# Expert stage of a hybrid backbone: TensorE in written order, gather and combination inside gate and up, and two adjacent weight rows of each 256 on a partition

## The chip, the cores and the metric

The kernel runs on one core of a Trainium2 chip. The metric is the device time of one execution in microseconds (us). A core has five engines, each with an instruction queue of its own that is worked off in order: TensorE (PE, matrix products; its weight loads are listed as PEld), VectorE (DVE), ScalarE (ACT), GpSimd (POOL) and SyncE (SP), which here mainly issues DMAs. Sixteen DMA engines move data between the memory outside (DRAM) and the core's own (SBUF). Matrix products land in PSUM.

## The reference

One layer of a backbone with a token-mixing half and an expert half, on 512 tokens of width 2048. Only the expert half concerns the change. Every token chooses one of four expert groups and two of the eight experts in it; an expert is a gated MLP of width 512:

```python
def _hier_moe(h, w_rg, b_rg, w_re, b_re, w_gate, w_up, w_down):
    # top-1 group, top-2 experts in it, weights wts; slots sorted by expert
    ...
    def expert_block(args):
        idx, e = args
        xb = h_pad[idx]
        return (jax.nn.silu(xb @ w_gate[e]) * (xb @ w_up[e])) @ w_down[e]
    ys = lax.map(expert_block, (buf_tok.reshape(n_blocks, MOE_BLOCK), blk_e))
    ys = ys.reshape(cap, d) * buf_w[:, None].astype(h.dtype)
    return jax.ops.segment_sum(ys, buf_tok, num_segments=t + 1)[:t]
```

Here `h` is the modulated, normalised stream (512 x 2048). The result is scaled by a row of modulation (`gt2`), added to the stream, and the stream is normalised once more for the output. All 32 experts' weights (32 x 3 matrices of 2048 x 512 in f32, 403 MB) are read in every run.

## The kernel before

The first two thirds of the kernel (modulation, input projection, three recurrent mixers, output projection) stay as they are. `out_more` loads two rows of the modulation, spread over all partitions, into `as2`; `route_tile` and `route_h2` multiply and add them to make `h2` (128 partitions x 4 token tiles x 2048). `route_slots` chooses the experts. Then comes `phase_moe`, the expert stage.

An expert's tokens are gathered into 64 slots. The work of the stage:

- `gather(q)` serves four experts at once ("quad" below). It makes a one-hot matrix `G` (tokens x 4 x 64 slots) on VectorE and multiplies `h2` by it on TensorE, in 16 chunks of 128 features. Each chunk is split into a rounded part `hh` (cast by ScalarE) and a rest `hl` (subtracted by VectorE, for odd chunks by GpSimd), each with two buffers; a chunk is 8 matmuls of 256 columns (L1685), and after two chunks VectorE copies the PSUM tile (`pc_`, three buffers) to `xg` (L1686). `xg` is one tile with one buffer.
- `gate_up(e)` multiplies the 64 slots by gate and up together: 16 features-chunks x 2 column halves = 32 matmuls into `pgu` (L1716). The halves `c` go to different 64-column parts of TensorE. ScalarE applies silu, VectorE multiplies (`sil_`).
- `turn(e)` transposes the activation (L1728) to `hT`.
- `down(pr, cols)` multiplies a pair of experts by w_down, 8 matmuls for each of four column blocks of 512 (L1740, `py`); VectorE scales (`yt`), ScalarE rounds (`yeh`), VectorE takes the rest (`yel`).
- `slots(pr)` makes the pair's one-hot matrix, its transpose `GT` (L1698, L1699) and the slots' weights (L1702).
- `combine()` adds a column block to the stream `x1`: for four token tiles two matmuls with `GT` into `pc_` (L1763) and an addition on VectorE (L1764).

A f32 matmul of `pgu` or `py` leaves two records in the trace, so one expert's gate/up has 64, and the profile's "x8" is four matmuls.

The weights go through a ring of ten slots of 1 MB (`slot`, `load`): each gate/up slot holds two feature rows of gate and of up on each partition, each down slot two row blocks. `load()` is called when a slot has been read; SyncE issues the DMA when the slot's last reader is done. SyncE's queue is in order.

What sets the order: the instructions of an engine are put in order by a list scheduler at build time, which takes ready work by priority, so the order in the program is not that of the source. In the stage before, a quad's gather runs while its first expert's gate/up runs, chunk by chunk ahead of it.

## Time and profile before

| | |
|---|---|
| median of 3 runs | 3124.62 us (3121.7 to 3134.05) |
| profiled execution | 3124.07 us; span from first to last instruction 3122.3 us |
| PE busy | 2810.3 us (90%) |
| DVE, ACT, POOL busy | 1633.1, 859.9, 812.2 us |
| DMA | 730.79 MB, mean 234 GB/s |
| one quad in the stage, 2261.60 to 2397.60 | PE busy 130.34 of 136.00 us, DMA 370 GB/s |
| gate/up matmuls (L1716) | 2048 records, 487.1 us busy |
| down matmuls (L1740) | 1024 records, 257.0 us busy |

Times of single instructions are counted from the span's start. "Busy" of TensorE includes the modelled ends of matmuls, so a stretch can be busy and still not dense. Rows of a wait name who waited and, behind the arrow, what came last. The expert stage begins at about 2010 us and lasts to the end.

### The profile page before, as it was taken

The numbers are of one execution on the slowest core, as the hardware profiler recorded it, in microseconds if no ns is written. First come the engines' busy times: TensorE is split into PE (matmuls) and PEld (weight loads), VectorE is DVE, ScalarE is ACT, GpSimd is POOL, SyncE is SP. The second block draws the span as 40 slices with busy tenths as digits, with TensorE's granted clock in tenths as the row PEclk, the third lists the DMA queues.
The fourth block names the chain that finished last, engine by engine and source line by source line (L and its number), as shares of the span: only waits on it lengthen the run. The fifth ranks groups of instructions, "written<-read, shape, count | busy, mean of one in ns | idle before, by whom it ended". The sixth has DMA issues, their size and how long they took to land. (4 is left out here: it accounts for less than half of the span.)

```text
span 3122.3 us, 50607 instructions
## 1 busy us (share of the span) xinstructions
PE 2810.3 (90%) x19241; PEld 1825.2 (58%) x19241; DVE 1633.1 (52%) x3215; ACT 859.9 (28%) x1570; POOL 812.2 (26%) x765
## 2 busy tenths in 40 slices
PE   5989998988989989889789888799999999999997
PEld 3478777777677766667556666644344343434432
DVE  4275657685675554455375656624343342434335
ACT  4142332346432233222132332412122120212202
POOL 2232222221433432433343443411011010101101
PEclk9999999989999999999989899899999999999999
DMA  8767878887543443443383323499999999999996
GB/s 305 272 191 217 248 221 265 246 258 210 136 110 97 104 108 98 105 107 82 103 266 98 116 70 100 154 365 369 409 342 385 362 343 410 342 409 342 382 369 247
DMA packets 526878, 730.79 MB, mean 234 GB/s; under 512 B 121042, under 2 KB 343808, under 8 KB 525220
## 3 DMA queue, kind: packets, MB, share of 16 engines
q1 hardware_dynamic: 362832, 640.77, 57.9%
q10 hardware_dynamic: 161927, 81.17, 10.2%
q0 software_dynamic: 1872, 5.57, 0.6%
q8 instruction: 154, 2.52, 0.3%
q14 instruction: 93, 0.75, 0.1%
HBM read 672.50 MB, written 54.93 MB: 233 GB/s over the span
## 5 line engine op out<-in xcount | busy, mean ns | idle before, releaser
L1716 PE MATMUL pgu<-ring,xg 128*64 128x512 f32 x2048 | 487.1, 599 | 0.0
L307 POOL TENSOR_TENSOR wl<-wr,wh 128x512 fp32r<-128x512 f32 x191 | 263.8, 1382 | 666.9 <-ACT wh L306 606.9
L329 PE MATMUL pl<-hil,wh 128*128 128x512 f32 x928 | 404.2, 436 | 4.6 <-ACT hil L241 3.7
L329 PE MATMUL pl<-lol,wh 128*128 128x512 f32 x928 | 375.9, 405 | 0.2
L329 PE MATMUL pl<-hil,wl 128*128 128x512 f32 x928 | 371.5, 400 | 1.1 <-POOL wl L307 1.1
L306 ACT CAST wh<-wr 128x512 fp32r<-128x512 f32 x292 | 179.6, 619 | 532.2 <-PE pl L329 290.6
L1682 POOL TENSOR_TENSOR hl<-h,hh 128x512 fp32r<-128x512 f32 x64 | 99.4, 1554 | 861.7 <-ACT hh L1681 861.7
L1716 PEld LDWEIGHTS pgu<-ring,xg 128*64 128x64 f32 x2048 | 137.3, 136 | 254.1 <-issue 236.0
L1740 PE MATMUL py<-ring,hT 128*64 128x512 f32 x1024 | 257.0, 598 | 0.0
L259 DVE SCALAR_TENSOR_TENSOR acc<-w,sil,acc 128x512 f32<-128x512 f32 x240 | 201.4, 868 | 55.6 <-DMA w<-in_w_ada_dram 54.0
L329 PEld LDWEIGHTS pl<-hil,wh 128*128 128x128 f32 x928 | 178.9, 193 | 60.5 <-issue 15.1
L329 PEld LDWEIGHTS pl<-hil,wl 128*128 128x128 f32 x928 | 178.7, 193 | 42.2 <-POOL wl L307 1.8
L329 PEld LDWEIGHTS pl<-lol,wh 128*128 128x128 f32 x928 | 179.7, 194 | 38.1 <-issue 6.4
L1681 ACT CAST hh<-h 128x512 fp32r<-128x512 f32 x128 | 134.4, 1092 | 120.1 <-PE pc__20645 L1685 2.7
L1740 PEld LDWEIGHTS py<-ring,hT 128*64 128x64 f32 x1024 | 85.8, 136 | 129.7 <-issue 125.1
L329 PE MATMUL pc<-hic,wl 128*128 128x256 f32 x496 | 146.0, 295 | 12.9 <-DVE wl L307 8.7
L329 PE MATMUL pc<-hic,wh 128*128 128x256 f32 x496 | 145.8, 295 | 5.9 <-ACT hic L241 3.2
L329 PE MATMUL pc<-loc,wh 128*128 128x256 f32 x496 | 144.9, 293 | 1.2 <-DVE loc L242 1.2
L1748 DVE SCALAR_TENSOR_TENSOR yt<-py,Wsl,g 128x512 f32<-128x512 f32 x64 | 48.1, 751 | 161.1 <-PE py L1740 158.4
L1749 ACT CAST yeh<-yt 128x512 fp32r<-128x512 f32 x64 | 39.6, 619 | 290.0 <-DVE yt L1748 290.0
L1410 POOL TENSOR_TENSOR wol<-wo,woh 128x512 fp32r<-128x512 f32 x56 | 76.0, 1361 | 160.3 <-PE acc L1413 100.6
L776 DVE TENSOR_TENSOR ptm<-Tm,Lay 64x1 f32<-64x1 f32 (+2 forms) x270 | 106.9, 396 | 16.9 <-DMA Lay<-s_ad 10.2
(2216 smaller groups left out, 5074.9 us busy)
## 6 DMA issues: line engine op xcount, KB each, us to landing
ring<-in_moe_w_gate_dram SPq DMA_DIRECT2D x256, 512.0 KB
ring<-in_moe_w_up_dram SPq DMA_DIRECT2D x256, 512.0 KB
ring<-in_moe_w_down_dram SPq DMA_DIRECT2D x128, 1024.0 KB
wr<-in_w_in_dram ACTq DMA_DIRECT2D x288, 256.0 KB
w<-in_w_ada_dram SPq DMA_DIRECT2D x256, 256.0 KB
w<-in_w_ada_dram SPq DMA_DIRECT2D x64, 512.0 KB
wo<-in_w_out_dram SPq DMA_DIRECT2D x56, 256.0 KB
rv_xk<-d_xk SPq DMA_DIRECT2D x36, 256.0 KB
```

The costliest lines, as they stand in the source:

```text
L259: nc.vector.scalar_tensor_tensor(acc, w, self.sil[:, k, 0:1], acc, op0=OP.mult, op1=OP.add)
L306: nc.scalar.copy(wh[:, :, :n], wr[:, :, :n])
L307: (nc.vector if q in self.wdve else nc.gpsimd).tensor_tensor(wl[:, :, :n], wr[:, :, :n], wh[:, :, :n].bitcast(F32), op=OP.subtract)
L329: nc.tensor.matmul(o[:n], a[:, k, :n], r, start=(q == k == i == 0), stop=(q == k == 3 and i == 2))
L776: nc.vector.tensor_tensor(pt_[:, :t, :t], Tm[:, :t, :t], Lay[:, :t, t].rearrange("q (o s) -> q o s", o=1).to_broadcast([64, t, t]), op=OP. ...
L1410: nc.gpsimd.tensor_tensor(wl, w, wh.bitcast(F32), op=OP.subtract)
L1681: nc.scalar.copy(hh, h)
L1682: (nc.gpsimd if k else nc.vector).tensor_tensor(hl, h, hh.bitcast(F32), op=OP.subtract)
L1716: nc.tensor.matmul(p[64 * c:64 * c + 64], x[:, k, 64 * (e % 4):64 * (e % 4) + 64], g[:, :, k % 2, 256 * c:256 * c + 256], start=(k == 0), ...
L1740: nc.tensor.matmul(py[64 * c:64 * c + 64], ht[2 * pr + c][:, f % 2, 64 * (f // 2):64 * (f // 2) + 64], wgt[2 * pr + c, (col[0] // 1024, f ...
L1748: nc.vector.scalar_tensor_tensor(yt, py, W, self.g2[:, col[0]:sum(col)], op0=OP.mult, op1=OP.mult)
L1749: nc.scalar.copy(yh, yt)
```

## The change

It does five things.

1. Every matmul and transpose of the stage is kept in the order in which the code writes it (`pin`, by the helpers `mm` and `tr`; in the profile all their instructions then have the helper's line). The other engines are still ordered by the scheduler.
2. The code is written in the wanted order: `gate_up(e, *work)` takes a list of (j, call) and makes the call behind feature pair j. The calls are steps of the gather (always two at once: 32 matmuls), the transpose of the expert before, the two parts of `slots`, and two combinations. The gather of the next four experts now begins inside the last gate/up of the quad (two pairs of steps) and ends inside the next one's (two more). For the first quad three steps stand before the first gate/up.
3. `xg` becomes eight tiles of two chunks, `xg0` to `xg7`, so that each can be written again as soon as its own readers are done. `as2`, which shares their memory, is cut into eight tiles, loaded by eight DMAs in place of two.
4. A gate/up slot now holds 256 consecutive rows of the matrix, rows 2p and 2p+1 of them on partition p, in place of rows 16p+2c and 16p+2c+1. Each DMA still moves 4 KB to a partition, now from 512 KB that lie together. The gather takes the matching features: every second column of a block of 256 (step 2) in place of every 16th.
5. `combine` takes the oldest column block and not the newest.

```diff
     def out_more(self):
-        self.as2 = self.xgp.tile([P, 2, D], F32, name="as2", tag="xg")
-        self.row_bc(self.as2[:, 0], 2)
-        self.row_bc(self.as2[:, 1], 1)
+        self.as2 = [[self.xgp.tile([P, 512], F32, name=f"as2_{j}{q}", tag=f"xg{4 * j + q}") for q in range(4)] for j in range(2)]
+        for j, ts in enumerate(self.as2):
+            for q, t in enumerate(ts):
+                self.nc.sync.dma_start(t, self.d_ada[1, 2 - j:3 - j, 512 * q:512 * q + 512].to_broadcast([P, 512]))
...
-                nc.sync.dma_start(w[:, j], I[nm][0, e].rearrange("(p k) c -> p k c", p=P)[:, 2 * c:2 * c + 2])
+                nc.sync.dma_start(w[:, j], I[nm][0, e, 2 * c * P:(2 * c + 2) * P].rearrange("(p k) c -> p k c", k=2))
...
+            pin = tc.keep_in_program_order
+            def mm(*a, **k):
+                pin(nc.tensor.matmul(*a, **k))
...
             def gather(q):
-                x = xg[q] = self.xgp.tile([P, KT, 256], F32, name="xg")
+                xg[q] = []
                 yield
                 for k0 in range(0, KT, 2):
+                    x = self.xgp.tile([P, 2, 256], F32, name=f"xg{k0 // 2}")
+                    xg[q].append(x)
                     p = ps.tile([P, 2, 256], F32, name="pc_", bufs=3)
                     for k in range(2):
-                        h = self.h2[:, :, k0 + k::KT]
+                        h = self.h2[:, :, k0 * P + k:(k0 + 2) * P:2]
...
-            def gate_up(e, gat=iter(())):
+            def gate_up(e, *work):
...
+                    load()
+                    for at, call in work:
+                        if at == j:
+                            call()
...
-                pr, col, yh, yl = ys.pop()
+                pr, col, yh, yl = ys.pop(0)
...
             for pr in range(NE // 2):
                 a = 2 * pr
-                gate_up(a, gather(pr // 2) if pr % 2 == 0 else iter(()))
-                if pr:
-                    down(pr - 1, COLS[:2])
-                else:
-                    slots(0)
-                turn(a)
-                gate_up(a + 1)
-                if pr:
-                    down(pr - 1, COLS[2:])
-                    slots(pr)
-                turn(a + 1)
-            down(pr, COLS)
-            combine()
+                sl = slots(pr)
+                if pr == 0:
+                    gat = gather(0)
+                    for _ in range(4):
+                        next(gat)
+                    gate_up(a, *((j, partial(next, gat, None)) for j in range(5)))
+                else:
+                    two = () if pr % 2 else ((0, partial(next, gat)),) * 2 + ((4, partial(next, gat)),) * 2
+                    gate_up(a, *two, (1, partial(turn, a - 1)), (2, combine), (5, combine))
+                    for col in COLS[:2]:
+                        down(pr - 1, col)
+                two = ()
+                if pr % 2 and a + 2 < NE:
+                    gat = gather(pr // 2 + 1)
+                    next(gat)
+                    two = ((3, partial(next, gat)),) * 2 + ((6, partial(next, gat)),) * 2
+                next(sl)
+                gate_up(a + 1, (0, partial(turn, a)), (1, combine), (2, partial(next, sl)), *two, (4, partial(next, sl)), (5, combine))
+                if pr:
+                    for col in COLS[2:]:
+                        down(pr - 1, col)
+            turn(a + 1)
+            combine()
+            combine()
+            for i, col in enumerate(COLS):
+                down(pr, col)
+                if i:
+                    combine()
+            combine()
```

How instructions move, at three places. First TensorE around the combination behind a pair's first two down blocks (`pc_<-yeh,GT` and `pc_<-yel,GT` are the combination's two matmuls, `pgu` gate/up, `ts<-ident,sil` the activation's transpose). Before:

```order
L1763 MATMUL pc__21745<-yel,GT 128x512
L1716 MATMUL pgu<-ring_21640,xg 64x512
L1763 MATMUL pc__21749<-yeh,GT 128x512
L1763 MATMUL pc__21749<-yel,GT 128x512
L1716 MATMUL pgu<-ring_21640,xg 64x512 x3
L1763 MATMUL pc__21851<-yeh,GT 128x512
L1763 MATMUL pc__21851<-yel,GT 128x512
L1716 MATMUL pgu<-ring_21647,xg 64x512 x4
```

One gate/up matmul stands alone between two parts of a combination, and three follow. At the same kind of place now:

```order
L1672 MATMUL pgu<-ring_21462,xg_21184 64x512 x4
L1675 MATMUL ts<-ident,sil__21586 128x128 x2
L1672 MATMUL pgu<-ring_21485,xg_21211 64x512 x4
L1672 MATMUL pc__21654<-yeh,GT 128x512
L1672 MATMUL pc__21654<-yel,GT 128x512
L1672 MATMUL pc__21658<-yeh,GT 128x512
L1672 MATMUL pc__21658<-yel,GT 128x512
...
L1672 MATMUL pgu<-ring_21492,xg_21282 64x512 x4
```

The combination's eight matmuls now stand together, and gate/up comes by four.

Second TensorE at a quad's gather (`pc_<-G,hh` and `pc_<-G,hl`, four matmuls for each part of a chunk). Before, inside the first gate/up of the quad:

```order
L1685 MATMUL pc__22172<-G,hh 128x256 x4
L1685 MATMUL pc__22172<-G,hl 128x256 x4
L1716 MATMUL pgu<-ring_21944,xg 64x512 x4
L1685 MATMUL pc__22172<-G,hh 128x256 x4
L1685 MATMUL pc__22172<-G,hl 128x256 x4
L1685 MATMUL pc__22205<-G,hh 128x256 x4
L1685 MATMUL pc__22205<-G,hl 128x256 x4
L1716 MATMUL pgu<-ring_21951,xg 64x512 x4
```

Now, the second block of four chunks in the same gate/up:

```order
L1672 MATMUL pgu<-ring_21279,xg_21393 64x512 x4
L1672 MATMUL pc__21496<-G,hh 128x256 x4
L1672 MATMUL pc__21496<-G,hl 128x256 x4
L1672 MATMUL pc__21496<-G,hh 128x256 x4
L1672 MATMUL pc__21496<-G,hl 128x256 x4
L1672 MATMUL pc__21523<-G,hh 128x256 x4
L1672 MATMUL pc__21523<-G,hl 128x256 x4
L1672 MATMUL pc__21523<-G,hh 128x256 x4
L1672 MATMUL pc__21523<-G,hl 128x256 x4
L1672 MATMUL pgu<-ring_21340,xg_21420 64x512 x4
```

Two chunks between gate/up groups have become four, in four blocks a quad in place of eight.

Third ScalarE from the last expert of a quad to the first of the next (`hh` the gather's casts, `sil` the activation, `yeh` the down's rounding, `hT` the transposed activation). Before:

```order
L1749 CAST yeh<-yt 128x512
L1681 CAST hh<-h_19608 128x512 x16
L1721 ACTIVATE sil__22337<-pgu 128x256
L1749 CAST yeh<-yt 128x512 x2
L1730 COPY hT_22415<-ts 128x256
```

Now:

```order
L1692 CAST hh<-h_19621 128x512 x8
L1736 ACTIVATE sil__22144<-pgu 128x256
L1764 CAST yeh<-yt 128x512 x2
L1692 CAST hh<-h_19621 128x512 x4
L1745 COPY hT_22257<-ts 128x256
L1692 CAST hh<-h_19621 128x512 x4
```

The sixteen casts of a gather stood in one run and now stand in three, around the activation and the rounding; both kernels' first run of casts in the stage is 18 long.

More of the change, by code (lines that the diff above doesn't have):

```diff
@@ L1684, in gather @@
                             for t in range(4):
-                                nc.tensor.matmul(p[:, k], hx[:, t], G[:, t].rearrange("p e s -> p (e s)"), start=(i == t == 0), stop=(i == 1 and t == 3))
-                    nc.vector.tensor_copy(x[:, k0:k0 + 2], p)
+                                mm(p[:, k], hx[:, t], G[:, t].rearrange("p e s -> p (e s)"), start=(i == t == 0), stop=(i == 1 and t == 3))
+                    nc.vector.tensor_copy(x, p)
                     yield
@@ L1705, in slots @@
                 gts[pr] = (GT, W)
-            def gate_up(e, gat=iter(())):
-                next(gat, None)
+                yield
+            def gate_up(e, *work):
                 x = xg[e // 4]
                 p = ps.tile([P, 2, 256], F32, name="pgu", bufs=2)
-                for k in range(KT):
-                    if k % 2 == 0:
-                        next(gat, None)
-                    g = wgt[e, k // 2]
-                    for c in range(2):
-                        nc.tensor.matmul(p[64 * c:64 * c + 64], x[:, k, 64 * (e % 4):64 * (e % 4) + 64], g[:, :, k % 2, 256 * c:256 * c + 256],
-                                         start=(k == 0), stop=(k == KT - 1), tile_position=(0, 64 * c))
-                    if k % 2:
-                        load()
+                for j in range(KT // 2):
+                    g = wgt[e, j]
+                    for k in range(2):
+                        for c in range(2):
+                            mm(p[64 * c:64 * c + 64], x[j][:, k, 64 * (e % 4):64 * (e % 4) + 64], g[:, :, k, 256 * c:256 * c + 256],
+                               start=(j == k == 0), stop=(j == 7 and k == 1), tile_position=(0, 64 * c))
+                    load()
+                    for at, call in work:
+                        if at == j:
+                            call()
                 s_ = mo.tile([P, 256], F32, name="sil_", bufs=2)
@@ L1727, in turn @@
                 for j in range(2):
[L1728 removed]
+                    tr(pt[:, j], hm[e][:, j * P:(j + 1) * P], self.ident)
                 ht[e] = mo.tile([P, 2, P], F32, name=f"hT{e % 2}", bufs=2 - e % 2)
@@ L1731, in turn, with down @@
                 del hm[e]
-            def down(pr, cols):
+            def down(pr, col):
                 W = gts[pr][1]
-                for col in cols:
-                    n = col[1]
-                    py = ps.tile([P, n], F32, name="py", bufs=2)
-                    for f in range(4):
-                        for c in range(2):
-                            nc.tensor.matmul(py[64 * c:64 * c + 64], ht[2 * pr + c][:, f % 2, 64 * (f // 2):64 * (f // 2) + 64], wgt[2 * pr + c, (col[0] // 1024, f // 2)][:, f % 2, col[0] % 1024:col[0] % 1024 + n],
-                                             start=(f == 0), stop=(f == 3), tile_position=(0, 64 * c))
-                    if col[0] % 1024:
-                        for _ in range(4):
-                            load()
-                    yt = mo.tile([P, n], F32, name="yt", bufs=1)
-                    yh = mo.tile([P, n], F32R, name="yeh", bufs=2)
-                    yl = mo.tile([P, n], F32R, name="yel", bufs=2)
-                    nc.vector.scalar_tensor_tensor(yt, py, W, self.g2[:, col[0]:sum(col)], op0=OP.mult, op1=OP.mult)
-                    nc.scalar.copy(yh, yt)
-                    nc.vector.tensor_tensor(yl, yt, yh.bitcast(F32), op=OP.subtract)
-                    combine()
-                    ys.append((pr, col, yh, yl))
+                n = col[1]
+                py = ps.tile([P, n], F32, name="py", bufs=2)
+                for f in range(4):
+                    for c in range(2):
+                        mm(py[64 * c:64 * c + 64], ht[2 * pr + c][:, f % 2, 64 * (f // 2):64 * (f // 2) + 64],
+                           wgt[2 * pr + c, (col[0] // 1024, f // 2)][:, f % 2, col[0] % 1024:col[0] % 1024 + n],
+                           start=(f == 0), stop=(f == 3), tile_position=(0, 64 * c))
+                if col[0] % 1024:
+                    for _ in range(4):
+                        load()
+                yt = mo.tile([P, n], F32, name="yt", bufs=1)
+                yh = mo.tile([P, n], F32R, name="yeh", bufs=2)
+                yl = mo.tile([P, n], F32R, name="yel", bufs=2)
+                nc.vector.scalar_tensor_tensor(yt, py, W, self.g2[:, col[0]:sum(col)], op0=OP.mult, op1=OP.mult)
+                nc.scalar.copy(yh, yt)
+                nc.vector.tensor_tensor(yl, yt, yh.bitcast(F32), op=OP.subtract)
+                ys.append((pr, col, yh, yl))
             def combine():
@@ L1762, in combine @@
                     for j, y in enumerate((yh, yl)):
-                        nc.tensor.matmul(p, gts[pr][0][:, t * P:(t + 1) * P], y, start=(j == 0), stop=(j == 1))
+                        mm(p, gts[pr][0][:, t * P:(t + 1) * P], y, start=(j == 0), stop=(j == 1))
                     nc.vector.tensor_tensor(self.x1[:, t, cs], self.x1[:, t, cs], p, op=OP.add)
```

16 lines of the change are left out of this document (10 added, 6 removed).

## The prediction

> **What bounds the kernel now.** I read the page first (who is busy, which chain ends last), then the expert stage in stretches of one expert, then the SyncE queue's waits, then single instructions in order of time.
>
> ```profile
> PE 2810.3 (90%) x19241; PEld 1825.2 (58%) x19241; DVE 1633.1 (52%) x3215; ACT 859.9 (28%) x1570; POOL 812.2 (26%) x765
> PE 32%; DVE 2%; ACT 1%; issue 0%; POOL 0%; ACTq 0%; POOLq 0%; DVEq 0%
> ```
>
> The chain that ended last is followed back through TensorE (PE) for 32% of the span, about 1000 us, which is the expert stage. There the work repeats every four experts (a "quad": one gather serves four). One quad, expert by expert:
>
> ```profile
> core 0: us, PE busy (x) PEld busy (x) DVE busy (x) ACT busy (x) POOL busy (x), PEclk, DMA share, GB/s
> 2261.60:2302.60 41.00, 41.00 (x219) 21.68 (x218) 23.49 (x29) 15.77 (x18) 11.47 (x8) 1.00 0.79 279
> 2302.60:2331.40 28.80, 27.21 (x126) 10.97 (x125) 8.09 (x18) 1.89 (x5) 0.00 (x0) 1.00 1.03 411
> 2331.40:2363.60 32.20, 30.59 (x127) 11.73 (x126) 9.40 (x20) 2.60 (x6) 0.00 (x0) 1.00 1.02 409
> 2363.60:2397.60 34.00, 31.54 (x143) 13.62 (x142) 12.71 (x20) 5.43 (x8) 0.92 (x1) 1.00 1.03 409
> 2261.60:2397.60 136.00, 130.34 (x609) 58.01 (x608) 53.70 (x84) 25.68 (x35) 12.40 (x9) 1.00 0.95 370
> ...
> SPq L1656 <- PE pgu L1716: 269.2, 141, 5.7
> ```
>
> A quad takes 136.0 us. Its weights (four experts, three matrices of 2048x512 f32) are 50.33 MB, and three of the four experts load at 409 to 411 GB/s with the 16 DMA engines full; at 410 the quad would take 122.8 us. In the first expert, where the gather stands, the rate falls to 279: the queue waits for TensorE to free ring slots (269 us over 141 waits). So TensorE is the bound and the transfers lie 13.2 us a quad below it. A TensorE gain counts fully up to there and no further.
>
> Where TensorE's 136.0 us go is seen in single instructions (start, duration, count):
>
> ```profile
> 2603.89 1.07 PE L1716 MATMUL pgu<-ring,xg 128*64 128x512 f32 x2
> 2605.56 1.93 PE L1716 MATMUL pgu<-ring,xg 128*64 128x512 f32 x6
> 2607.42 0.50 PE L1763 MATMUL pc__24233<-yeh,GT 128*128 128x512 f32 x1
> 2607.76 0.40 PE L1763 MATMUL pc__24233<-yel,GT 128*128 128x512 f32 x1
> 2608.09 1.94 PE L1716 MATMUL pgu<-ring,xg 128*64 128x512 f32 x8
> 2611.53 10.52 PE L1716 MATMUL pgu<-ring,xg 128*64 128x512 f32 x48
> 2623.36 1.93 PE L1740 MATMUL py<-ring,hT 128*64 128x512 f32 x4
> 2627.54 7.08 PE L1740 MATMUL py<-ring,hT 128*64 128x512 f32 x28
> ...
> 2711.12 7.09 PE L1716 MATMUL pgu<-ring,xg 128*64 128x512 f32 x32
> ...
> 2739.94 1.07 PE L1716 MATMUL pgu<-ring,xg 128*64 128x512 f32 x2
> ...
> 2692.18 0.64 PE L1685 MATMUL pc__24653<-G,hl 128*128 128x256 f32 x4
> 2692.66 0.64 PE L1685 MATMUL pc__24686<-G,hh 128*128 128x256 f32 x4
> ...
> 2709.43 0.39 PE L1763 MATMUL pc__24782<-yeh,GT 128*128 128x512 f32 x1
> 2709.66 0.39 PE L1763 MATMUL pc__24782<-yel,GT 128*128 128x512 f32 x1
> ```
>
> 2603.89 and 2739.94 are the same place a quad apart: 136.05. A gate/up or down matmul leaves two records and uses half the columns; two on opposite halves run together in a slot. From x8 to x48 is ten slots: (10.52-1.94)/10 = 0.858 us. But x6 takes as long as x8 (1.93) and x28 as long as x32 (7.08, 7.09): **a matmul without its partner costs a whole slot**.
>
> A quad's dense work: 64 gate/up and 32 down slots, 96 x 0.858 = 82.4; 128 gather matmuls at 0.48/4 = 0.12, 15.4; 64 combination matmuls at 0.235, 15.0; transposes and slot weights 3.5 (an estimate, 2 x 1.05 + 2 x 0.66 + small). Together 116.3. The other 19.7 us are lone halves, changes of mode and waits.
>
> **The change, part by part.** *Lone halves.* The old order has seven lost slots a quad: two in gate/up (1 and 3 around a combination), five in down. The new one issues gate/up by 4 and down by 16, halves alternating: -7 x 0.858 = -6.0.
>
> *Fewer excursions.* Leaving gate/up and coming back costs: two slots 1.72, but 2605.56 to 2607.42 is 1.86; two combination matmuls 0.47, but 2607.42 to 2608.09 is 0.67. That is 0.34 each. The order has 26 a quad before and 20 now: -2.0; 20 x 0.34 = 6.8 stay.
>
> *Waits that go.* TensorE's named waits in the stage:
>
> ```profile
> PE ts L1702 <- ACT GT L1699: 5.4, 8, 0.7
> PE pc__23615 L1763 <- ACT yeh L1749: 0.9, 1, 0.9
> PE ts L1728 <- DVE sil__24215 L1722: 0.9, 1, 0.9
> ...
> PE ts L1728 <- DVE sil__26597 L1722: 0.9, 1, 0.9
> ```
>
> In the whole stage the activation's transpose waits 0.9 in 22 rows, of which the first and the last stand above, about three a quad (2.8); the first combination behind a down waits 0.6 to 0.9 in 16 rows like the second, two a quad (1.3); the slot weights 0.7 once. That is 4.8, and what is left of the 19.7 is 19.7-6.0-8.8 = 4.9. After, a down of 6.9 us or one to two gate/up groups of 1.72 stand between, and ScalarE and VectorE need 1 to 2.3 there: taken as gone; if half stays, 2.4 a quad.
>
> *Waits that come.* TensorE's order is now fixed, so two places are exposed. First the gather, in four blocks of 32 matmuls (3.84 us), with hh and hl in two buffers each. The rows for their producers, and for accesses with other steps:
>
> ```profile
> L1681 ACT CAST hh<-h x128: 1057/1096/1141, 2010.6 to 2964.6; 128x512 fp32r<-128x512 f32 x128
> L1682 DVE TENSOR_TENSOR hl<-h,hh x64: 1022/1414/1439, 2011.7 to 2962.8; 128x512 fp32r<-128x512 f32 x64
> L1682 POOL TENSOR_TENSOR hl<-h,hh x64: 1515/1546/1690, 2012.8 to 2965.8; 128x512 fp32r<-128x512 f32 x64
> ...
> L1749 ACT CAST yeh<-yt 128x512 fp32r<-128x512 f32 x50 | 30.9, 619 | 231.0 <-DVE yt L1748 231.0
> L1750 DVE TENSOR_TENSOR yel<-yt,yeh 128x512 fp32r<-128x512 f32 x50 | 34.4, 689 | 14.3 <-ACT yeh L1749 14.3
> L307 POOL TENSOR_TENSOR wl<-wr,wh 128x512 fp32r<-128x512 f32 x191 | 263.8, 1382 | 666.9 <-ACT wh L306 606.9
> ...
> L1270 DVE TENSOR_TENSOR gl_qd<-gl_q,gl_ex x6: 277/279/2774, 1771.2 to 1774.7; 128x128 f32<-128x128 f32 x6
> L1271 POOL TENSOR_TENSOR gl_kd<-gl_k,gl_ex x7: 446/449/504, 1770.3 to 1773.4; 128x128 f32<-128x128 f32 x7
> L1610 DVE TENSOR_TENSOR G<-iota,rt_pos 128x256 fp32r<-128x256 f32 x20 | 13.8, 748 | 0.0
> ```
>
> Today h2 is read with a step of 16 floats, and a cast takes 1.10 against 0.62 for unit step. The new rows make the step 2. The runs at L1270 and L1271 end with their step-of-2 piece, and VectorE's costs what its neighbours cost (277 to 280 ns), GpSimd's stays below 0.51. ScalarE has no such row; I take its unit-step end, 0.62 of 0.62 to 1.10, because the other two engines show no penalty; VectorE's subtraction 0.7 to 1.4, GpSimd's 1.4. In a block the first two chunks are ready (their casts stand right behind the block before). The third's cast starts when TensorE has read the first: 0.48+0.62+0.9 = 2.0 against TensorE's arrival at 2.4: no wait. The fourth: 1.44+0.62+1.4 = 3.46 against 3.36, some 0.5 with the handovers (an estimate). Four blocks: 2.0 a quad. With today's times: the third 0.48+1.10+1.41 = 2.99, 0.6 to 0.9 late, the fourth another 0.4: 1.3 a block, 5.2 a quad.
>
> Of ScalarE, the Trainium skill says (page "SBUF — State Buffer", section "Door 1: The DMA port swizzle") that memory is fetched in lines of 16 bytes and runs at full rate with at least two hits per line, four floats being the furthest free step. Today's step of 64 bytes paying 1.10 against 0.62 agrees; a step of 8 bytes would be free, and the sum by it is the one I take; were it not so, the sum would be the first rival's.
>
> Second, the four one-hot masks of the next gather (G, 4 x 0.75 = 3.0 us on VectorE) now stand ahead of a combination's four additions in the quad's first expert. They begin some 0.8 us behind the gather block, end at 3.8, and the first addition (some 0.7) gives the first of three PSUM buffers back at 4.5; TensorE reaches the fourth partial sum at 1.86+3x0.47 = 3.3. That is a wait of 1.2. Together 3.2.
>
> A quad after: 116.3+6.8+3.2 = 126.3, which is 9.8 less (136.05) and still above the transfers' 122.8.
>
> *Row order of the weights.* Each packet stays 4 KB; only the distance between partitions falls from 32 KB to 4 KB. The down weights already lie 8 KB apart, and no stretch above with both kinds leaves 409 to 411. I take no change; bounds: 390 to 412.
>
> *as2 in eight pieces.* Six more issues on SyncE ahead of the next operand load:
>
> ```profile
> 1738.01 0.86 SPq L284 DMA_DIRECT2D as<-d_ada  x2
> 1738.92 0.42 SPq L1394 DMA_DIRECT2D yk<-d_y  x1
> 1742.25 17.09 SPq L1403 DMA_DIRECT2D wo<-in_w_out_dram  x2
> ```
>
> 6 x 0.43 = 2.6 us into a gap of 2.9 between the yk load's issue and the next: nothing, 2.6 at most if yk is awaited.
>
> *Start and end.* Three gather steps instead of one and a half precede the first gate/up (24 x 0.12 = 2.9 later, but gone from inside). The first quad has three of those transposes (2.8) and some four lost slots (3.4): -6. Behind the last gate/up three lost slots go: -3 (2.6 plus a change of mode).
>
> Sum: 7 x 9.8 + 6 + 3 = 77.6. The profiled execution took 3124.07 (span 3122.3 and 1.8 around it; the median of the runs is 3124.62): **3046.5**.
>
> **Rivals.**
> 1. *The step of 2 is no faster*: a quad 5.2-2.0 = 3.2 longer, the first one too: 3046.5+26 = 3072. For it: ScalarE has no row. Against: L1270, L1271. Chance 0.12.
> 2. *The transfers become the bound.* At 126.3 they have 3.5 us to spare; below 50.33/126.3 = 398 GB/s they decide. The two experts without a gather (24 slots, 16 combination matmuls and some 2 us each, 53 together) draw on the ring, since their loads take 61.4; the ring's ten 1 MB slots are 25 us of loads, so a full ring holds. At 390 a quad is 129.1: 3066; at 380, 132.4: 3089; 370 would be no change. 512 KB read in one piece by all engines is in no row of the stage. Chance 0.16, with 0.04 of it near 370, within 0.5%.
> 3. *Slower: a producer behind other work on its engine holds the fixed order.* Were the first casts of a block behind the pair's yeh casts rather than ahead, each block would begin with cast and subtraction, 1.10+1.41+0.2 = 2.7 us more, and with today's times 1.3 besides. It decides from 13.0 us of waits a quad (9.8+3.2), 2.95 a block besides the masks' 1.2; at 4.0 a block a quad is 116.3+6.8+17.2 = 140.3: 3124+7x4.2 = 3153. Against: ScalarE's new order keeps two casts ahead (its first run is 18, two more than a gather has). Chance 0.04.
> 4. *Nothing waits at all*: 122.9 a quad, just what the transfers allow: 3020. Chance 0.06.
>
> My forecast has the other 0.62. Over 0.5% (15.6 us, about what a measurement of this kernel can tell from no change) faster: all but 0.04 and 0.04. The range of 8 in 10 goes from just above rival 4, 3026, past rival 1 and most of rival 2, to 3086; the forecast's own is 3033 to 3064 (half of the named waits staying adds 17, a gather block without waits takes 14).
>
> **What would show it.** Right: quads of 125 to 128 us, no wait for sil or yeh on TensorE, gate/up in runs of 8 records or multiples, DMA near 400 GB/s in every expert, hh at 0.62 to 0.68. Wrong: hh at 1.1; TensorE waiting for the ring's DMAs; waits of over 2 us at a gather block or behind G; quads above 133.

## The result, and the profile after

The changed kernel takes 3049.56 us, the median of four runs (3042.62 to 3053.76), against 3127.84 for the kernel before beside it (3121.7 to 3134.05): a ratio of 0.9747 with a 95% interval of 0.9718 to 0.9777. Forecast were 3046.5 with 3026 to 3086. The profiled execution took 3046.72 (span 3045.0), 77.35 less than the profiled one of before.

The stage cut into its first quad, the six that repeat, and the rest up to the span's end; first before, then after. Columns: stretch, length, busy time of each engine with its instructions, granted clock, DMA share, GB/s.

```profile
2018.60:2125.51 106.91, 103.08 (x507) 46.54 (x506) 35.77 (x56) 24.94 (x32) 12.47 (x9) 1.00 0.95 363
2125.51:2942.31 816.80, 782.52 (x3649) 348.08 (x3649) 322.11 (x504) 154.48 (x205) 74.67 (x49) 1.00 0.96 373
2942.31:3122.30 179.99, 156.98 (x687) 66.17 (x686) 75.17 (x127) 39.01 (x70) 20.10 (x17) 0.96 0.80 310
```

```profile
2020.18:2121.34 101.16, 99.87 (x512) 45.57 (x513) 29.36 (x53) 18.84 (x31) 13.02 (x10) 1.00 0.94 365
2121.34:2877.43 756.09, 749.14 (x3650) 338.52 (x3648) 298.42 (x504) 118.49 (x204) 62.88 (x48) 1.00 1.01 400
2877.43:3045.00 167.57, 147.73 (x660) 61.32 (x656) 71.75 (x127) 32.45 (x66) 14.48 (x13) 0.96 0.88 350
```

The six quads give 60.7 us (136.13 to 126.02 each), the first 5.8, the last with the end 12.4; together 78.9, and the stage begins 1.6 later. The DMA engines are nearly full over whole quads now (1.01; before 0.96, where the experts without a gather showed 1.02 to 1.03). The first and the last expert of one quad, the quad, and the chain line of the page:

```profile
2247.20:2282.40 35.20, 34.62 (x180) 17.18 (x178) 16.35 (x25) 7.29 (x12) 5.24 (x4) 1.00 0.97 382
...
2335.90:2373.00 37.10, 36.53 (x192) 18.58 (x190) 15.63 (x27) 7.88 (x13) 5.23 (x4) 1.00 1.03 409
2247.20:2373.00 125.80, 124.65 (x610) 56.86 (x608) 49.73 (x84) 19.74 (x34) 10.47 (x8) 1.00 1.01 400
...
PE 29%; DMA 2%; POOL 1%; ACT 1%; DVE 1%; issue 0%; ACTq 0%; POOLq 0%; DVEq 0%; SPq 0%
```

The gather's 3.84 us blocks stand in the first and the fourth expert, so the quad's long experts are 35.20 and 37.10, where before one of 41.00 stood. TensorE's record in the quad's first expert (start, duration, count; in brackets a wait and what ended it):

```profile
2248.97 0.74 PE L1672 MATMUL pc__22195<-G,hh 128*128 128x256 f32 x4
...
2251.95 0.64 PE L1672 MATMUL pc__22222<-G,hh 128*128 128x256 f32 x4
2252.87 0.74 PE L1672 MATMUL pc__22222<-G,hl 128*128 128x256 f32 x4 [0.29 <-POOL hl L1693]
2253.54 1.94 PE L1672 MATMUL pgu<-ring,xg 128*64 128x512 f32 x8
...
2257.64 0.50 PE L1672 MATMUL pc__22266<-yeh,GT 128*128 128x512 f32 x1
...
2259.15 0.50 PE L1672 MATMUL pc__22278<-yeh,GT 128*128 128x512 f32 x1
2259.49 0.40 PE L1672 MATMUL pc__22278<-yel,GT 128*128 128x512 f32 x1
2259.81 3.65 PE L1672 MATMUL pgu<-ring,xg 128*64 128x512 f32 x16
```

Gate/up comes in x8 and x16, the transpose behind it waits for nothing, and the only named wait is that of the block's last chunk for GpSimd's `hl`: 2251.95 + 0.48 = 2252.43, and it starts at 2252.87, 0.44 late. In the six quads no wait for `sil`, `yeh` or `GT` is listed on TensorE any more. The casts of the same kernel, all 128 of them (shortest, median and longest in ns):

```profile
L1692 ACT CAST hh<-h x128: 647/661/685, 2008.3 to 2895.5; 128x512 fp32r<-128x512 f32 x128
```

### The profile page after: what moved, and what is told of

It is laid out like the page before. It is cut to its first block, busy times and chain, and to the rows that moved or that the text cites. A ratio compares the mean times of both kernels' runs of the same rounds, so it can differ in the third digit from the quotient of the medians.

```text
span 3045.0 us, 50599 instructions
## 1 busy us (share of the span) xinstructions
PE 2764.3 (91%) x19241; PEld 1811.1 (59%) x19241; DVE 1597.2 (52%) x3215; ACT 811.3 (27%) x1570; POOL 796.0 (26%) x765
## 3 DMA queue, kind: packets, MB, share of 16 engines
q1 hardware_dynamic: 363696, 640.77, 58.8%
## 5 line engine op out<-in xcount | busy, mean ns | idle before, releaser
L1672 PE MATMUL pgu<-ring,xg 128*64 128x512 f32 x2048 | 480.6, 600 | 0.0
L1693 POOL TENSOR_TENSOR hl<-h,hh 128x512 fp32r<-128x512 f32 x64 | 83.9, 1311 | 809.7 <-ACT hh L1692 779.4
L1672 PE MATMUL py<-ring,hT 128*64 128x512 f32 x1024 | 230.4, 593 | 2.4 <-DMA ring<-in_moe_w_down_dram 2.4
L259 DVE SCALAR_TENSOR_TENSOR acc<-w,sil,acc 128x512 f32<-128x512 f32 x240 | 201.7, 870 | 58.5 <-DMA w<-in_w_ada_dram 57.6
L329 PEld LDWEIGHTS pl<-hil,wh 128*128 128x128 f32 x928 | 178.8, 193 | 60.7 <-issue 14.6
L1672 PEld LDWEIGHTS py<-ring,hT 128*64 128x64 f32 x1024 | 76.7, 137 | 149.4 <-issue 141.9
L1692 ACT CAST hh<-h 128x512 fp32r<-128x512 f32 x128 | 84.7, 663 | 193.7 <-POOL hl L1693 14.8
L776 DVE TENSOR_TENSOR ptm<-Tm,Lay 64x1 f32<-64x1 f32 (+2 forms) x270 | 105.5, 391 | 20.3 <-DMA Lay<-s_ad 10.1
L1693 DVE TENSOR_TENSOR hl<-h,hh 128x512 fp32r<-128x512 f32 x64 | 53.2, 830 | 112.0 <-ACT hh L1692 109.5
```

The source lines that it names most:

```text
L259: nc.vector.scalar_tensor_tensor(acc, w, self.sil[:, k, 0:1], acc, op0=OP.mult, op1=OP.add)
L329: nc.tensor.matmul(o[:n], a[:, k, :n], r, start=(q == k == i == 0), stop=(q == k == 3 and i == 2))
L776: nc.vector.tensor_tensor(pt_[:, :t, :t], Tm[:, :t, :t], Lay[:, :t, t].rearrange("q (o s) -> q o s", o=1).to_broadcast([64, t, t]), op=OP. ...
L1672: pin(nc.tensor.matmul(*a, **k))
L1692: nc.scalar.copy(hh, h)
L1693: (nc.gpsimd if k else nc.vector).tensor_tensor(hl, h, hh.bitcast(F32), op=OP.subtract)
```

## The experiments

The main theory: TensorE bounds the stage; fixed runs of gate/up with even halves, fewer excursions, and producers moved behind long work make the gain, and the new rows keep the gather's blocks from waiting. Its rivals: the rows, as larger pieces, load faster; a fixed order alone is the gain; the transfers are the bound.

Ahead of the stage the kernels differ in nothing but the tiles and loads of `as2`, and in the profiled executions the first gate/up still begins anywhere from 2014 to 2029 us. That is as much as the runs of one kernel differ, so quads of the trace separate kernels finer than the times do. Quads without a range are one quad of the six.

### Rows and order apart

Old rows in the changed kernel:

```diff
-nc.sync.dma_start(w[:, j], I[nm][0, e, 2 * c * P:(2 * c + 2) * P].rearrange("(p k) c -> p k c", k=2))
+nc.sync.dma_start(w[:, j], I[nm][0, e].rearrange("(p k) c -> p k c", p=P)[:, 2 * c:2 * c + 2])
...
-h = self.h2[:, :, k0 * P + k:(k0 + 2) * P:2]
+h = self.h2[:, :, k0 + k::KT]
```

> The changed kernel with the old layout of the gate and up slots (rows 16p+2c and 16p+2c+1 on partition p, gather with a step of 16 floats); the order on every engine is that of the changed kernel. Theory: the weights load at the same rate, but the gather's casts are again at 1.06 to 1.14 us and the subtractions at 1.4 to 1.55, so each of a quad's four gather blocks waits some 0.8 to 1.3 us more: quads of 128.5 to 130 us in place of 125.8, and 3070 to 3083 in place of 3049.6. Rival 1, the casts have slack in the blocks too: quads within 0.5 us of 125.8, 3045 to 3056. Rival 2, most of the gain comes from the rows (as 512 KB pieces that load faster): quads of 132 or more, above 3095, with the DMA rate below 400 GB/s in every expert.

Measured: 3079.9 (3068.88 to 3082.52), 0.9859 of before (0.9838 to 0.988). Its quad, its casts, and its gather block at the place shown above:

```profile
2249.95:2379.06 129.11, 125.83 (x611) 56.30 (x609) 52.02 (x84) 26.59 (x34) 12.25 (x8) 1.00 0.99 390
...
L1692 ACT CAST hh<-h x128: 1060/1108/1152, 2004.9 to 2915.7; 128x512 fp32r<-128x512 f32 x128
...
2251.77 0.73 PE L1672 MATMUL pc__22195<-G,hh 128*128 128x256 f32 x4
...
2254.84 0.74 PE L1672 MATMUL pc__22222<-G,hl 128*128 128x256 f32 x4 [0.38 <-DVE hl L1693]
...
2256.38 0.74 PE L1672 MATMUL pc__22222<-G,hl 128*128 128x256 f32 x4 [0.33 <-POOL hl L1693]
2257.05 1.94 PE L1672 MATMUL pgu<-ring,xg 128*64 128x512 f32 x8
```

The block lasts 2257.05-2251.77 = 5.28 against 2253.54-2248.97 = 4.57. Four blocks make 2.8 of the 3.3 us by which the quad is longer; the other 0.5 stands at the combination behind the second block (2.76 against 2.25). This was the first rival of the prediction, priced there at 3.2 a quad and 26 us; the run shows 3.3 a quad, and its median lies 30 us above the changed kernel's (31 to 35 by the ratios to before). The waits are for `hl`, so the rows work through the step with which cast and subtraction read `h2` (the cast 1.108 against 0.661, VectorE's subtraction at the median 1.09 against 0.69, GpSimd's 1.53 against 1.30); that they leave the transfers' rate alone is shown further down.

The other half alone, the new rows in the kernel before:

```diff
-nc.sync.dma_start(w[:, j], I[nm][0, e].rearrange("(p k) c -> p k c", p=P)[:, 2 * c:2 * c + 2])
+nc.sync.dma_start(w[:, j], I[nm][0, e, 2 * c * P:(2 * c + 2) * P].rearrange("(p k) c -> p k c", k=2))
...
-h = self.h2[:, :, k0 + k::KT]
+h = self.h2[:, :, k0 * P + k:(k0 + 2) * P:2]
```

> The kernel before with the new layout of the gate and up slots and the gather's step of 2, and nothing else. Theory: in the old order two chunks of gather stand between two gate/up groups, so cast and subtraction have 1.7 us of cover for each pair and nothing waits for them; shorter casts then gain nothing: quads of 135.5 to 136.3, 3118 to 3130 (before: 3127.8). Rival 1, the casts hold the old order up as well: quads of 133 or less, 3105 or below. Rival 2, pieces of 512 KB in one stretch load slower: the three experts without a gather fall below 405 GB/s, and the time rises by less than 10 us, since TensorE is the bound.

Measured: 3118.09 (3107.3 to 3125.95, ten runs), 0.9975 of before (0.996 to 0.9989).

```profile
2266.89:2402.30 135.41, 130.14 (x609) 57.90 (x608) 50.10 (x84) 19.52 (x35) 10.43 (x9) 1.00 0.95 371
```

A small gain, 0.7 us a quad: the quad lies a little below the theory's range, the time at its edge. The pieces of two chunks inside gate/up come every 3.97 us in both kernels, so they were not late. The difference stands in one place a quad, ahead of the first gate/up, where three chunks stand together and the third one's `hl` is late; first the kernel before, then this run:

```profile
2260.69 0.74 PE L1685 MATMUL pc__22107<-G,hl 128*128 128x256 f32 x4 [0.38 <-DVE hl L1682]
```

```profile
2266.06 0.66 PE L1685 MATMUL pc__22107<-G,hl 128*128 128x256 f32 x4
```

From the first of these chunks to gate/up it is 3.98 us before and 3.31 here. The rows are worth 0.7 with the old order and 3.3 with the new one, where four chunks stand together four times a quad and the third and fourth must be made inside the block.

### A fixed order without the new code, and the new code without a fixed order

```diff
+            pin = tc.keep_in_program_order
+            def mm(*a, **k):
+                pin(nc.tensor.matmul(*a, **k))
...
-                                nc.tensor.matmul(p[:, k], hx[:, t], G[:, t]...
+                                mm(p[:, k], hx[:, t], G[:, t]...
```

(on the kernel before, and so for all matmuls and transposes of the stage)

> The kernel before with its TensorE instructions kept in the order in which its code stands, and nothing else (old rows, one xg tile). Theory: a fixed order alone costs: the code calls gate/up directly behind the gather step that it reads, so TensorE waits eight times a quad for the copy of a PSUM tile to xg (some 2.1 us each, 17 in all), and four to seven more for transposes, slot weights and downs that stand behind their producers; lost slots go (-6). Quads of 143 to 150, 3175 to 3225. Rival: keeping gate/up together is what pays, wherever the rest stands: quads below 132, under 3095. Half way (133 to 140) would say that both are of one size.

Measured: 3205.43 (3203.64 to 3211.09), 1.0262 of before (1.0239 to 1.0286). Its quad; its largest wait in the stage (us in total, times, longest); and one place of it:

```profile
2287.39:2434.19 146.80, 130.84 (x608) 59.16 (x608) 49.58 (x84) 26.04 (x34) 12.15 (x9) 0.97 0.88 343
...
PE pgu L1671 <- DVE xg L1693: 86.8, 64, 1.6
...
2292.88 1.94 PE L1671 MATMUL pgu<-ring,xg 128*64 128x512 f32 x8 [1.44 <-DVE xg L1693]
```

Gate/up waits 64 times, eight a quad, for the chunk just gathered to be copied to `xg`. That is 10.9 us a quad by name, of the size of the whole loss (10.7). Not all of that loss is the order's: the quad shown ran at a granted clock of 0.97, and the one at 1.00 (2579.72 to 2724.43) took 144.71, a loss of 8.7.

```diff
-            pin = tc.keep_in_program_order
+            pin = lambda i: i
```

(on the changed kernel)

> The changed kernel's code, rows and tiles, but TensorE's order left to the scheduler, as on the other engines. Theory: the order is the gain. The scheduler again breaks gate/up up: as built, a quad has nine lost slots (9 x 0.858 = 7.7 us) and 31 excursions out of gate/up or down where the changed kernel has 20 (11 x 0.34 = 3.7), and TensorE reaches the activation's transpose, the slot weights and the first combination behind a down some 0.9 us too early again (about 9 a quad). So quads of 135 to 140 and 3115 to 3150, the time of before or somewhat more. Rival: the places at which the code calls gather, transpose and combination carry the gain, and the scheduler takes them over: quads of 126 to 130, 3050 to 3080.

Measured: 3158.25 (3152.25 to 3163.38), 1.0109 of before (1.0083 to 1.0135). Its quad and a row of TensorE's record:

```profile
2273.35:2414.48 141.13, 135.69 (x610) 58.75 (x609) 48.64 (x85) 19.59 (x34) 10.42 (x8) 1.00 0.92 357
...
2296.91 0.44 PE L1675 MATMUL ts<-ident,sil__22387 128*128 128x128 f32 x2 [0.94 <-DVE sil__22387 L1737]
```

Both time and quad lie a little above the theory's range. Counted in the trace, the quad of 141.13 has 31 excursions (11 more than the changed kernel's, 3.6 us) and eight slots more than 96 (6.9 us), and TensorE waits 4.9 us by name for `sil`, `GT` and `yeh`, which the changed kernel doesn't; together 15.4, of the size of the 15.3 by which the quad is longer. So each half of "a written order" costs when it stands alone: against the 136.05 of before, the fixed order 10.7 us a quad and the new code 5.1. Together they gain about 10.

### What a lone matmul costs

```diff
+                    kc = [(k, c) for k in range(2) for c in range(2)]
+                    if j in (3, 6):
+                        kc.sort(key=lambda v: v[1])
-                    for k in range(2):
-                        for c in range(2):
+                    for k, c in kc:
```

> The changed kernel with the four matmuls of feature pairs 3 and 6 of every gate/up sorted by column half (half 0 twice, then half 1 twice), nothing else. Each sorted group leaves a matmul without its partner, so a quad has 8 lost slots. Theory: each costs 0.858 us, 6.9 a quad: quads of 132.0 to 133.0 us in place of 125.8, 3099 to 3110. Rival: a matmul without a partner costs half a slot, 0.43, and the seven lost slots of the order before were not 6.0 but 0 to 3 us: quads of 125.8 to 129.5, 3050 to 3080.

Measured: 3046.48 (3042.14 to 3053.64), 0.9759 of before (0.9731 to 0.9787), and the same undisturbed quad as the changed kernel (the mean of six is 126.3 against 126.0). The expectation counted lost slots by adjacency, and the theory fails: the sorted groups cost nothing. A run of twelve matmuls with a sorted group at its start, up to what follows it:

```profile
2247.79:2373.62 125.83, 124.69 (x611) 56.78 (x609) 49.72 (x84) 19.79 (x34) 10.45 (x8) 1.00 1.01 402
...
2318.69 5.38 PE L1672 MATMUL pgu<-ring,xg 128*64 128x512 f32 x24
2324.00 0.50 PE L1672 MATMUL pc__22647<-yeh,GT 128*128 128x512 f32 x1
```

5.31 us are the six slots of twelve matmuls (6 x 0.858 = 5.15) and the 0.15 that leaving gate/up costs; seven slots would be 6.0. So a matmul of one half goes ahead while the other half's next one still waits. What remained of the theory was the uneven run, like the x28 in the profile before: fourteen matmuls, six on one half and eight on the other. The next kernel makes such runs: the last matmul of a group is held back until behind the combination.

```diff
+                    late = any(at == j and call is combine for at, call in work)
+                    for k, c in ((0, 0), (0, 1), (1, 0)):
+                        half(k, c)
+                    if not late:
+                        half(1, 1)
+                        load()
                     for at, call in work:
                         if at == j:
                             call()
+                    if late:
+                        half(1, 1)
+                        load()
```

(`half(k, c)` is the matmul as it was)

> The changed kernel with the last matmul of a group held back until behind the combination, at both combinations of every gate/up: eight runs of gate/up between two other kinds of work end with one matmul too few on half 1, and the next ones have one too many. Counted by runs (a run takes as many slots as its fuller half has matmuls) a quad has 103 slots in place of 96. Theory, after sorted halves cost nothing: the halves queue separately inside a run, and what costs is a run with uneven halves, 0.858 a slot: 7 x 0.858 = 6.0, quads of 131.3 to 132.3 and 3093 to 3102. By the same count the kernel before has 5 lost slots a quad (4.3 us), not the 7 that adjacency gave. Rival: the halves also run across the work between (the eight matmuls of a combination do not end a pair), or a lone matmul costs half a slot: quads of 125.8 to 129, 3047 to 3075.

Measured: 3096.18 (3090.93 to 3102.17), 0.9922 of before (0.9903 to 0.9942).

```profile
2260.87:2392.59 131.72, 130.58 (x611) 57.75 (x608) 49.71 (x84) 19.78 (x34) 10.44 (x8) 1.00 0.98 383
...
2269.49 1.93 PE L1672 MATMUL pgu<-ring,xg 128*64 128x512 f32 x6
2271.35 0.51 PE L1672 MATMUL pc__22262<-yeh,GT 128*128 128x512 f32 x1
```

Three matmuls (x6) take 1.86 us, as four do, and the quad is 5.9 us longer for 7 lost slots: 0.85 each. The price of the prediction holds, and its count doesn't: by runs the order of before has 101 slots a quad in place of 96, five lost and not seven.

### What an excursion costs

```diff
-            def combine():
+            def combine(ts=range(4)):
...
-                for t in range(4):
+                for t in ts:
...
+            c1, c2 = partial(combine, (0, 1)), partial(combine, (2, 3))
...
-                    gate_up(a, *two, (1, partial(turn, a - 1)), (2, combine), (5, combine))
+                    gate_up(a, *two, (1, partial(turn, a - 1)), (2, c1), (3, c2), (5, c1), (6, c2))
-                gate_up(a + 1, (0, partial(turn, a)), (1, combine), (2, partial(next, sl)), *two, (4, partial(next, sl)), (5, combine))
+                gate_up(a + 1, (0, partial(turn, a)), (0, c1), (1, c2), (2, partial(next, sl)), *two, (4, partial(next, sl)), (5, c1), (6, c2))
```

> The changed kernel with each combination inside gate/up cut in two (token tiles 0 and 1 behind one feature pair, 2 and 3 behind the next): 28 excursions out of gate/up a quad in place of 20, the same matmuls. Theory: an excursion costs 0.34 (0.38 by the quad of 125.8): 2.7 to 3.0 a quad, so 128.3 to 129.0 and 3069 to 3076. Rival 1: what was put down to excursions is waiting for the three PSUM buffers of a combination's four partial sums, which halves do not need: quads of 125.8 or less, 3040 to 3052. Rival 2: an excursion is 0.6 or more (the first matmuls behind a change are late too): quads above 130.5.

Measured: 3053.28 (3048.11 to 3061.39), 0.9776 of before (0.9749 to 0.9802).

```profile
2256.65:2383.22 126.57, 125.40 (x611) 55.35 (x608) 50.39 (x84) 19.74 (x34) 10.49 (x8) 1.00 1.01 399
...
2265.29 1.94 PE L1672 MATMUL pgu<-ring,xg 128*64 128x512 f32 x8
2267.16 0.50 PE L1672 MATMUL pc__22266<-yeh,GT 128*128 128x512 f32 x1
...
2268.28 1.94 PE L1672 MATMUL pgu<-ring,xg 128*64 128x512 f32 x8
```

The expectation miscounted: three of the new halves fall in with a transpose or a gather block, so 25 excursions are left and not 28. A half's excursion takes 2268.28-2267.16 = 1.12 for four matmuls of 0.235 (0.18 over), and the group ahead of it 1.87 for 1.72 (0.15 over): 0.33, as predicted. Five more would make 1.65, and the quad is 0.77 longer. The rest is given back: a whole combination takes 2259.81-2257.64 = 2.17, which is 0.29 over its eight matmuls, where a half has 0.18; the fourth partial sum (2259.15 to 2259.49, 0.34 in place of 0.235) waits about 0.1 for the first PSUM buffer. Eight times 0.11 to 0.13 is 0.9 to 1.0 a quad. So both mechanisms are there, each with a part, though the time lies in neither one's range.

### What the transfers allow

> The changed kernel without the gather of all quads but the first (every quad reads the first one's gathered tokens; masks, casts and gather matmuls of the other seven are left out). TensorE then has some 107 us of work a quad (125.8 less 15.4 of matmuls, 1.8 of waits and 1.4 of excursions), so the transfers set the time and their own rate is measured. Theory: 409 to 410 GB/s, 122.8 to 123.1 a quad, 3025 to 3032: the changed kernel lies 3 us a quad above its transfers. Rival 1: the new layout sustains less, 400 as the changed kernel shows over a quad: 125.8, 3045 to 3050, and the changed kernel was bound by transfers and not by TensorE. Rival 2: above 415, the 409 to 411 of the experts before was a limit of the ring and not of the engines: quads below 121.3, under 3018.

```diff
                 es = [4 * q + i for i in range(4)]
+                if q:
+                    xg[q] = xg[0]
+                    for _ in range(9):
+                        yield
+                    return
```

Measured: 3025.21 (3023.37 to 3030.49), 0.9689 of before (0.9667 to 0.9711). The same with the old rows (the diff under "Rows and order apart"):

> The kernel that gathers for the first quad alone (masks, casts and gather matmuls of the other seven left out), now with the old rows 16p+2c and 16p+2c+1 on a partition. With the new rows its quads took 123.2 to 124.0 us, 406 to 408.6 GB/s, TensorE waiting for the ring's DMAs. Theory: the rows do not change the rate of the transfers: quads of 123.0 to 124.2, 3021 to 3030. Rival 1, pieces of 512 KB in one stretch are faster: quads of 125 or more here, above 3036. Rival 2, they are slower: quads of 122.3 or less here, under 3018.

Measured: 3029.82 (3025.77 to 3032.38), 0.9701 (0.9681 to 0.972). Six quads of the first kernel with TensorE's largest wait (for the ring's DMAs), and then six of the second:

```profile
2114.36:2855.66 741.30, 688.74 (x2883) 249.20 (x2880) 212.95 (x384) 54.83 (x108) 0.00 (x0) 0.99 1.03 409
...
PE py L1672 <- DMA ring<-in_moe_w_down_dram: 65.4, 70, 2.2
```

```profile
2117.11:2856.21 739.10, 685.00 (x2884) 248.87 (x2881) 212.96 (x384) 54.83 (x108) 0.00 (x0) 1.00 1.03 409
```

409 GB/s with either layout, and 123.6 and 123.2 us a quad (single quads of the first, 123.2 to 124.0, lie a little above the theory's): the rows do not change the rate, and the changed kernel's 400 over a quad is what TensorE asks for. It lies 2.5 us a quad above its transfers (126.02 against 123.55).

### A version with fewer excursions

```diff
-gate_up(a, *two, (1, partial(turn, a - 1)), (2, combine), (5, combine))
+gate_up(a, *two, (1, partial(turn, a - 1)), (1, combine), (5, combine))
...
-gate_up(a + 1, (0, partial(turn, a)), (1, combine), (2, partial(next, sl)), *two, (4, partial(next, sl)), (5, combine))
+gate_up(a + 1, (1, partial(turn, a)), (1, combine), (1, partial(next, sl)), *two, (5, partial(next, sl)), (5, combine))
```

> The changed kernel with the calls inside gate/up put together: transpose and first combination behind pair 1, and in the second expert also the first part of slots there, the second part with the second combination behind pair 5. 12 excursions a quad in place of 20, the same matmuls. Theory: 8 x 0.34 to 0.38 = 2.7 to 3.0 go, so TensorE would need 122.8 to 123.1, and the transfers at 409 to 410 GB/s allow 122.8 to 123.1: quads of 122.8 to 123.6, 3028 to 3036. Rival 1, the transfers cannot keep 409 over a whole quad (they moved 400 over a quad, while TensorE was the bound): quads stay at 125 to 126, 3045 to 3050. Rival 2, work put side by side waits for its producers (the one transpose buffer, the additions): quads of 124 to 127 with named waits on TensorE.

Measured: 3041.06 (3035.11 to 3043.66), 0.9745 of before (0.9722 to 0.9767), quads of 124.7 to 125.4. That lies between theory and first rival. One of the causes stands in TensorE's record, at a combination behind the slot weights:

```profile
2289.95 0.48 PE L1672 MATMUL pc__22512<-yeh,GT 128*128 128x512 f32 x1
...
2292.40 1.08 PE L1672 MATMUL pgu<-ring,xg 128*64 128x512 f32 x4
```

2292.40-2289.95 = 2.45 where a combination took 2.17 above: the fourth partial sum comes late. The second cause is the transfers, as the next kernel shows. It turns the two around, `(5, combine), (5, partial(next, sl))`:

> The merged kernel with the second part of slots behind the second combination and not ahead of it (the two copies of slot weights on VectorE then no longer stand ahead of the combination's additions), nothing else. In the merged kernel the combination behind the slot weights took 2.45 us against 2.17, twice a quad, 0.56. Theory: that goes, but the transfers (123.2 to 124.0 a quad without a gather) and the ring, which runs empty in the two experts without gather (a first gate/up group 0.5 late in the merged kernel), take back most: quads of 124.2 to 124.8, 3033 to 3041, 0.2 to 0.5% below the changed kernel beside it. Rival: TensorE is still the bound: quads of 124.2 or below, 0.6% or more below the changed kernel.

> The changed kernel itself once more, on the chip of this call, to compare the merged kernels with it: 3043 to 3055, quads of 125.8 to 126.6.

Measured: 3044.57 (3039.73 to 3046.66), 0.9745 of before (0.9728 to 0.9762); the changed kernel beside it 3045.35 (3043.14 to 3051.5), 0.976 (0.9743 to 0.9778). The times don't tell the two apart, and the forecast of 3033 to 3041 missed; the profiled execution of the turned kernel also begins the stage 10 us later (2026.45 against 2016.46). The traces do: six quads of the turned kernel,

```profile
2126.49:2874.79 748.30, 738.23 (x3650) 342.00 (x3648) 297.22 (x504) 118.66 (x204) 62.70 (x48) 1.00 1.02 404
```

are 7.8 us shorter than the changed kernel's 756.09 (and 8.2 shorter than its 756.50 in the run beside it), 124.7 a quad. The turn did what it was for: the combination takes 2.09 there, up to the slot weights. In the stretch from 2120 to 2880 us TensorE's weight loads wait for the ring's down weights, in the changed kernel and then in the turned one,

```profile
PEld py L1672 <- DMA ring<-in_moe_w_down_dram: 1.1, 4, 0.6
```

```profile
PEld py L1672 <- DMA ring<-in_moe_w_down_dram: 9.4, 7, 2.4
```

and all rows that wait for the ring sum to 4.9 us and 16.8, 2.0 a quad more. The largest stand in one run a quad, behind the third expert's last combination; here its first matmuls in one quad and a weight load in it:

```profile
2327.68 3.65 PE L1672 MATMUL pgu<-ring,xg 128*64 128x512 f32 x16
2334.05 0.20 PEld L1672 LDWEIGHTS py<-ring,hT 128*64 128x64 f32 x4 [1.03 <-DMA ring<-in_moe_w_down_dram]
```

Its 16 slots take 15.10 (up to the transposes at 2342.78) where the other runs of 16 in the quad take 13.89; in the six quads this run takes 15.1 to 17.0, 1.6 more than 13.89 in the mean. Eight excursions fewer would be 2.6 us a quad; 1.3 of it is left in the quad and 1.6 is lost in this run, so the excursions go as priced, and weights that come late at this place take back about half. The quad stands 1.1 to 1.5 above the transfers' own 123.2 to 123.6.

## Why the prediction was right, point by point

- *TensorE is the bound and the transfers lie below.* Right. The floor was taken as 122.8 at 410 GB/s; the kernels with one gather show 123.2 to 123.6 at 409. The second rival (transfers become the bound) fell: with the gather gone the same rows load at 409, well above its 398. The fourth (nothing waits, 122.9) is shorter than the transfers take. That a TensorE gain counts fully down to the transfers didn't hold: of the 2.6 us that the turned kernel's excursions give, 1.3 were left while its quad still stood 1.1 or more above them, since in one run a quad the ring's weights come late.
- *A quad.* 126.3 predicted, 125.80 at its cleanest and 126.02 the mean of six; 9.8 less predicted, 10.1 measured. The six quads gave 60.7 us where 58.8 were forecast. The 126.3 is dense work, 20 excursions and waits that come; how the gain splits into lone halves and waits doesn't enter it.
- *Lone halves, -6.0.* The price (0.858) is right, the count isn't: adjacency gave seven, runs give five, -4.3. The waits that go were taken as the rest, so what is too much here is missing there, and the sum is not touched.
- *Excursions, 26 to 20 at 0.34.* 0.33 measured.
- *Waits that go, -4.9.* No wait for `sil`, `yeh` or `GT` is left in the six quads. What went in all is, by subtraction, 10.25 (136.05 to 125.80) + 2.8 of waits that came - 4.3 - 2.0 = 6.8. That the prediction's rest of 4.9 met its 4.8 of named waits was chance: it left two rows of the profile before out, each once a quad,

```profile
PE pc__22039 L1763 <- DVE x L1764: 0.5, 1, 0.5
PE pc__22901 L1685 <- DVE hl L1682: 0.4, 1, 0.4
```

  and the second costs 0.7, as the run with the new rows alone shows. With them 6.0 of the 6.8 are named; where the other 0.8 was, no run here measured by itself.
- *Waits that come, 3.2.* 2.8 in sum, with another make-up. The gather blocks wait 4 x 0.44 = 1.8 (2.0). The masks ahead of the additions, 1.2, failed: four masks took 2.09 us and not 3.0, as the row below shows, the first addition follows them at once, and the combination behind them takes 2.25 against 2.17 elsewhere.

```profile
2268.69 2.09 DVE L1611 TENSOR_TENSOR G<-iota,rt_pos 128x256 fp32r<-128x256 f32 x4
2270.70 0.68 DVE L1778 TENSOR_TENSOR x<-x,pc__22357 128x512 f32<-128x512 f32 x1
```

  In its place stands about 0.12 in each of eight combinations, 1.0, which the prediction didn't have: three buffers for four partial sums. That the two errors are of one size is luck.
- *The cast, 0.62 taken out of 0.62 to 1.10.* 0.661. The Trainium skill (page "SBUF — State Buffer", section "Door 1: The DMA port swizzle") has steps of up to four floats free and farther ones not; 0.661 at a step of 2, near the 0.62 of unit step, and 1.108 at a step of 16 agree. The page says this of SBUF and names no engine there; that it holds for ScalarE is what these rows show.
- *Row order, no change of rate.* Right: 409 with both layouts.
- *Start and first quad, -6.* The first quad is 5.8 shorter. The stage's start, 1.6 later, can't be told from its spread (the changed kernel once more: 2016.5). *The end, -3:* 1.8, from 60.3 us behind the start of the last gate/up record (3062.0) to 58.5.
- *Rival 3, a fixed order held up by producers.* It didn't come as described (no block of the changed kernel begins late). A fixed order held up by a producer exists all the same, with another waiter: in the old code's order gate/up waits for VectorE's copy to `xg`, 146.8 a quad. The new code has at least one group of gate/up between a gather step and its reader, and in its six quads no wait for `xg` is listed.

## What to carry to other kernels

An order written out by hand paid here only where the code also puts each reader some work behind its producer; pinning an order that wasn't written for it, and writing one that isn't pinned, both cost (+2.6% and +1.1%). Where TensorE changes between column halves and full width, count by runs: a run costs as many slots as its fuller half, whatever the sequence inside, plus 0.33 us for each time it is left and resumed. Before going on to cut such costs, take the work of the bound engine away in one run and read what the transfers allow: here 2.5 us a quad were left, and half of them could be had in the quads, too little to show in the time.

## What the runs showed of the hardware

Halves queue apart: two matmuls of one half in a row don't hold up the other half (0 us for eight sorted groups a quad), and the pairing ends where full-width work comes between (0.85 us for each lost slot). Of this the Trainium skill (page "TensorEngine Tiling (Array Packing)", section "Key Properties") says that tiles work independently and that a change of tiling mode drains the engine; both agree with these runs, where leaving and resuming gate/up took 0.33 us together.

VectorE's subtraction takes 0.69 us alone and 1.01 where it overlaps GpSimd's by 0.46. In the changed kernel's six quads all 24 without an overlap take 0.69 and all 24 with 0.45 to 0.47 of it 1.00 to 1.01; one that overlapped by 0.71, in the run with the new rows alone, took 1.26. A gather block:

```profile
2250.49 0.69 DVE L1693 TENSOR_TENSOR hl<-h,hh 128x512 fp32r<-128x512 f32 x1 [0.97 <-ACT hh L1692]
2252.36 1.01 DVE L1693 TENSOR_TENSOR hl<-h,hh 128x512 fp32r<-128x512 f32 x1 [0.48 <-ACT hh L1692]
...
2251.50 1.32 POOL L1693 TENSOR_TENSOR hl<-h,hh 128x512 fp32r<-128x512 f32 x1 [11.46 <-ACT hh L1692]
```
